# Cross attention with heads 0 and 2 first, and the square sums of the turned residual in the second MLP set

## The chip, the cores and the metric

The kernel runs on one core of one Trainium2 chip. The metric is the device time of one execution in microseconds (us): 706.7 is the median of three executions of the kernel before (706.44, 706.7 and 707.56). The profile was taken in a further execution. The engines are named as in the profile: PE multiplies matrices, PEld is its weight load, DVE and ACT work element by element, POOL does a few such steps and issues some transfers, SP issues the others.

## The reference

One decoder block over 512 tokens of width 1024, in float32, with a memory of 256 tokens. Two mixers side by side, cross attention to the memory, an MLP with squared ReLU, and a norm ahead of each. The change touches what follows the mixers:

```python
hc = rms_norm(x, g_cross[l])
mem_n = rms_norm(mem, g_mem[l])
x = x + memory_cross_attention(hc, mem_n, w_cq[l], w_ckv[l], w_co[l])
hm = rms_norm(x, g_mlp[l])
x = x + jnp.square(jax.nn.relu(hm @ w_up[l])) @ w_down[l]
return rms_norm(x, g_final)
```

`memory_cross_attention` has 4 heads of width 256: q = h w_cq, scores against 256 keys, a softmax, the product with the values, and w_co.

## The kernel before

A tile has 128 partitions. Activations lie transposed, 8 tiles of 128 features by 512 tokens. Each float32 operand is split into a high and a low part (`split`, L118: ACT casts the high part in L120, DVE subtracts it in L121), and every product is three matmuls, high by high, high by low, low by high (`mm3`, L113, so that the PE rows of the profile are nearly all L114, L115 and L116). A matmul over 256 columns that follows others of its kind starts 0.12 us after the one before, one over 512 columns 0.23 us after it. PE executes in the order in which the program is written. The other engines' instructions are put in order by a planner at build time, which takes an instruction ahead of others written earlier if it is ready sooner by its own estimate; on the chip each engine then keeps that order. Waits between engines are put in for every dependency, also where a buffer is used anew.

`tick` (L333) counts pieces of PE work: `tile_mm` ticks once for 3 matmuls of 512 columns, `block_product` once for 6 of 256 columns. `after(n, fn)` queues a function for n ticks from now; it is written into PE's order at that tick. `flush` writes out what is still queued.

**The query projection.** `cross_query(n)` makes the queries of heads 2n and 2n+1 with seven block products in place of eight (`seven`, L849). Its result has four quadrants: "11" and "12" are the first head with tokens 0 to 255 and 256 to 511, "21" and "22" are the second head with the same halves. Each of the seven products is 24 matmuls, 4 ticks. In `ORDER` "11" is finished after the fourth product (A12), "22" after the fifth (s3), "12" after the sixth (s4), and "21" after the seventh (A22). `finish` takes a quadrant from a PSUM tile to its two parts in the tile `s`: by a `split`, or, where the sign is negative ("22" and "21"), by ACT in L889 and DVE in L890. So the first head of each set is complete one product ahead of the second. The three PSUM tiles x, y, z have the tag `sc`, of which there are three buffers; "21" is read from y.

**Cross attention.** `cross_scores(h)` (L769) has two steps j, each of 12 matmuls into one PSUM tile: j = 0 are tokens 0 to 255, j = 1 the others. After each come a maximum on DVE (L780, L784), two exponentials on ACT (L785), a reciprocal (L786) and two scalings on ACT (L789). `cross_transpose(h)` (L793) turns the result by 8 PE transposes and splits it into `mfac` tiles. `cross_out(h)` (L805) multiplies it with the values in two steps of 6 matmuls over 512 columns, each into an `acc` or the `av` tile, and splits the result into `xg`, the operand of the output projection. The two scores of the first set are written into the second `cross_query`: at tick 2 head 1, at tick 7 head 0. After the second `cross_query` come, in PE's order: scores of 3, out of 1, scores of 2, transposes of 3, out of 0, out of 3, and then the output projection `co` with the transposes of 2 at its tick 2 and the out of 2 at its tick 7. `projection` (L603) starts with the input tiles that are there (`early`) for three output tiles, and adds the `late` ones when they are made.

**The MLP.** Eight up sets of seven block products each and four down products alternate (two sets, one down). The first set has its own order, `FIRST_ORDER`: A11, s1, A12, s2, s4, s3, A22. After s1, s2 and s3 ACT copies a PSUM tile aside (L857, L859, L865), and a later product goes on in the tile that was copied. `finish` there is a ReLU and a square on ACT (L998, L999). Meanwhile the residual is turned so that tokens lie on partitions: `turn(i, t)` (L934), written into PE's order at ticks 5 to 8 (i = 0) and 10 to 13 (i = 1) of the first set, makes 4 PE transposes, one copy by ACT (L939) into a `vr` buffer, and a square sum on ACT (`square_sum`, L931, the work being in L932). The `vr` buffers are those of the residual itself, so that no copy of i = 0 can be written before the fourth turn has read it. After the last turn DVE combines the sums (L943 to L946); they scale the down products (L954).

Of the kernel before, what the change touches and what calls it, by code (L numbers as in the profile page):

```python
# [21 lines left out]
NT = T // P  # L22
# [10 lines left out]
MEMIN, EARLY, LATE = 16, [4, 5, 6, 0, 1], [2, 7, 3]  # L33
WARM = 8
ON_POOL = (1, 3, 5, 7), (1, 3, 5)
STAT1, STATM, TURN = 16, 20, 5
RIGHT_START, RIGHT_SPACE = 12, 10
CO_ORDER = 0, 4, 1, 5, 2, 6, 3, 7
PARTS = "A11", "A12", "A21", "A22"
# [12 lines left out]
def block_kernel(ctx: ExitStack, tc: tile.TileContext, x0g, xT, memT, wv, wm, wst, wcq, wdn, wckv, wpool, vecs, csts, idn, gfin, out):  # L52
# [18 lines left out]
    def nm(s):  # L71
        uid[0] += 1
        return f"{s}_{uid[0]}"
# [7 lines left out]
    def sb(tag, shape, bufs, dt=F32):  # L81
        if tag in MID_TAGS and not late:
            return mid["pool"].tile(shape, dt, tag=tag, name=nm(tag), bufs=bufs)
        if tag in STAGE_TAGS and not late:
            return stage.tile(shape, dt, tag=tag, name=nm(tag), bufs=bufs)
        p = apool if tag in EARLY_TAGS else late["pool"] if tag in LATE_TAGS else pool
        return p.tile(shape, dt, tag=tag, name=nm(tag), bufs=bufs)

    def tmp(dt=F32):
        return sb("tmp", [P, T], 3 if late else 10, dt)  # L90

    def small(n=1):
        return sb("small", [P, 4], 24)[:, :n]

    def pair(tag, bufs):
        return sb(tag, [P, 2, T], bufs, F32R)

    def ps(tag, bufs):
        return psum.tile([P, T], F32, tag=tag, name=nm(tag), bufs=bufs)

    def acc():
        return ps("acc", 2)
# [10 lines left out]
    def mm3(o, lh, ll, rh, rl, start, stop, free=False):  # L113
        nc.tensor.matmul(o, lh, rh, start=start, stop=False, skip_group_check=free)  # L114
        nc.tensor.matmul(o, lh, rl, start=False, stop=False, skip_group_check=free)  # L115
        nc.tensor.matmul(o, ll, rh, start=False, stop=stop, skip_group_check=free)  # L116


    def split(hi, lo, src, eng=V):
        S.copy(hi, src)  # L120
        eng.tensor_tensor(lo, src, f(hi), op=ALU.subtract)  # L121
# [172 lines left out]
    def after(steps, fn, *args):  # L294
        heapq.heappush(due, (clock[0] + steps, uid[0], fn, args))
        uid[0] += 1

    def run_due():
        while due and due[0][0] <= clock[0]:
            _, _, fn, args = heapq.heappop(due)  # L300
            fn(*args)
# [6 lines left out]
    def flush():  # L308
        while due:
            clock[0] = max(clock[0], due[0][0])  # L310
            run_due()

    def tile_mm(o, w, rhs, ks=range(KC), first=True, last=True):
        ks = list(ks)
        for n, k in enumerate(ks):
            c = slice(k * P, (k + 1) * P)
            mm3(o, w[0][:, c], w[1][:, c], rhs[k][0], rhs[k][1],
                first and n == 0, last and n == len(ks) - 1)
            tick()
# [33 lines left out]
    def W(*key):  # L353
        return weights(where[key])
# [248 lines left out]
    def projection(key, rhs, early, late, done, between=None, order=range(KC)):  # L603
        held = []
        for m in order[:3]:
            w = W(key, m)
            o = ps("sc", 3)
            tile_mm(o, w, rhs, early, True, False)
            held.append((o, w))
        if between:  # L610
            between()
        for m, (o, w) in zip(order, held):
            tile_mm(o, w, rhs, late, False, True)
            done(m, o)
        for m in order[3:]:
            o = acc()
            tile_mm(o, W(key, m), rhs, early + late)
            done(m, o)
# [148 lines left out]
    cross_o = {}  # L767

    def cross_scores(h, tag, bufs):  # L769
        es = []  # L770
        for j in range(NT // 2):
            o = ps(tag, bufs)
            for b in range(2):
                i = 2 * j + b
                tb = slice(i * P, (i + 1) * P)
                for c in range(2):
                    q, k = st["cq", 2 * h + c], st["mk", 2 * h + c]
                    mm3(o[:, b * M:(b + 1) * M], q[0][:, tb], q[1][:, tb], k[0], k[1], c == 0, c == 1)
            mx, sm = small(2), small(2)
            V.tensor_reduce(mx, o.rearrange("p (b m) -> p b m", b=2), axis=AX.X, op=ALU.max, negate=True)  # L780
            e = tmp()
            for b in range(2):
                c, r = slice(b * M, (b + 1) * M), st["r1"][2 * j + b]
                V.tensor_tensor(mx[:, b:b + 1], mx[:, b:b + 1], r, op=ALU.mult)  # L784
                S.activation(e[:, c], o[:, c], AF.Exp, bias=mx[:, b:b + 1], scale=r, accum_out=sm[:, b:b + 1])  # L785
            V.reciprocal(sm, sm)  # L786
            for b in range(2):
                c = slice(b * M, (b + 1) * M)
                S.activation(e[:, c], e[:, c], AF.Copy, scale=sm[:, b:b + 1])  # L789
            es.append(e)  # L790
        st["p", h] = es

    def cross_transpose(h):  # L793
        pt = pair("mfac", 6), pair("mfac", 6)
        for j, e in enumerate(st["p", h]):
            tr = ps("tr", 2)
            for c in range(MT):
                for b in range(2):
                    nc.tensor.transpose(tr[:, (2 * c + b) * P:(2 * c + b + 1) * P],
                                        e[:, b * M + c * P:b * M + (c + 1) * P], ident)  # L800
            src = tr.rearrange("p (c t) -> p c t", c=MT)
            split(pt[0][:, :, j * M:(j + 1) * M], pt[1][:, :, j * M:(j + 1) * M], src)
        st["pt", h] = pt

    def cross_out(h):  # L805
        pt = st["pt", h]
        for dc in range(2):
            o = ps("av", 1) if (h, dc) in ((0, 0), (3, 1)) else acc()
            m = 2 * h + dc
            c = slice((m % 4) * P, (m % 4) * P + P)  # L810
            for i in range(MT):
                vh, vl = st["mv", m // 4, i]
                mm3(o, vh[:, c], vl[:, c], pt[0][:, i, :], pt[1][:, i, :], i == 0, i == MT - 1)
            pr = pair("xg", 8)
            split(pr[:, 0, :], pr[:, 1, :], o)
            cross_o[m] = (pr[:, 0, :], pr[:, 1, :])
# [59 lines left out]
    def cross_query(n):  # L876

        def store(m, p):
            st["cq", m] = p

        q = quads("s", 6, store, 4 * n)

        def finish(c, t, sign):
            hi, lo = q[c]
            t = two(t)
            if sign > 0:
                split(hi, lo, t)
            else:
                S.activation(hi, t, AF.Copy, scale=sign)  # L889
                V.scalar_tensor_tensor(lo, t, sign, f(hi), op0=ALU.mult, op1=ALU.subtract)  # L890

        seven("cq", n, rcross, finish, *(ps("sc", 3) for _ in range(3)), tmp(), tmp())

    cross_query(0)
    after(2, cross_scores, 1, "acc", 2)
    after(7, cross_scores, 0, "acc", 2)
    after(23, cross_transpose, 1)
    after(26, cross_transpose, 0)
    cross_query(1)
    flush()  # L900
    cross_scores(3, "sc", 3)
    cross_out(1)
    cross_scores(2, "sc", 3)
    cross_transpose(3)
    cross_out(0)
    cross_out(3)
    after(2, cross_transpose, 2)
    after(7, cross_out, 2)


    right = Right(G_MLP, "mix", 8, "s", 6)
# [12 lines left out]
        first.close()  # L924
        late["pool"] = ctx.enter_context(tc.tile_pool(name="late", bufs=1))

    projection("co", cross_o, [0, 1, 2, 3, 6, 7], [4, 5], done_co, renew, CO_ORDER)
    sums = sb("sums", [P, 32], 1)
    rows = {}

    def square_sum(t, i, col):  # L931
        S.activation(tmp(), rows[t, i], AF.Square, accum_out=sums[:, col:col + 1])  # L932

    def turn(i, t):  # L934
        o = ps("tr", 2) if t % 2 else acc()
        for j in range(4):
            nc.tensor.transpose(o[:, j * P:(j + 1) * P], res[4 * i + j][:, t * P:(t + 1) * P], ident)
        rows[t, i] = sb("vr", [P, T], 8)
        S.copy(rows[t, i], o)  # L939
        square_sum(t, i, NT * i + t)  # L940
        if i and t == NT - 1:
            v = sums[:, :NT]
            V.tensor_tensor(v, v, sums[:, NT:2 * NT], op=ALU.add)  # L943
            V.tensor_scalar(v, v, 1.0 / D, EPS, op0=ALU.mult, op1=ALU.add)
            V.reciprocal(sums[:, 2 * NT:3 * NT], v)
            V.tensor_scalar(sums[:, 6 * NT:7 * NT], sums[:, 2 * NT:3 * NT], -1.0, None, op0=ALU.mult)  # L946

    for i in range(2):
        for t in range(NT):
            after(TURN + (NT + 1) * i + t, turn, i, t)  # L950

    def gather(t, i, o, c=slice(T), minus=False):
        y, o, n = rows[t, i][:, c], o[:, c], (6 if minus else 2) * NT + t
# [249 lines left out]
```

## Time and profile before

The profiled execution took 702.63 us, of which the span from the first to the last instruction is 700.8; the median of the three executions without a profile is 706.7.

| | DVE | ACT | POOL | PEld |
|---|---|---|---|---|
| busy us in the span | 549.2 | 478.1 | 91.1 | 603.7 |
| share of the span | 78% | 68% | 13% | 86% |

The stages around the change, in us from the span's start:

| stage | from | to |
|---|---|---|
| second `cross_query`, with the scores of the first | 280.60 | 309.7 |
| scores, transposes and outs up to `co` | 309.7 | 329.6 |
| `co` | 329.6 | 376.9 |
| first up set | 376.9 | 401.9 |
| second up set | 401.9 | 421.9 |
| the rest of the MLP and the final norm | 421.9 | 700.8 |

A row of the timeline gives start, duration, engine, line, operation, the tiles (output first, then inputs), shapes and a count; at its end, in brackets, stands how long the engine had been idle and what released it. Durations of matmuls overlap, so their starts tell the pace. The windows view gives a stretch, its length, and for each engine the busy time and the number of instructions in it; then the granted PE clock as a share of full speed, the busy share of the transfer engines and GB/s.

### The profile page before, as it was taken

The numbers are of one execution on the slowest core, as the hardware profiler recorded it, in microseconds if no ns is written. First come the engines' busy times: TensorE is split into PE (matmuls) and PEld (weight loads), VectorE is DVE, ScalarE is ACT, GpSimd is POOL, SyncE is SP. The second block draws the span as 40 slices with busy tenths as digits, with TensorE's granted clock in tenths as the row PEclk, the third lists the DMA queues.
The fourth block names the chain that finished last, engine by engine and source line by source line (L and its number), as shares of the span: only waits on it lengthen the run. The fifth ranks groups of instructions, "written<-read, shape, count | busy, mean of one in ns | idle before, by whom it ended". The sixth has DMA issues, their size and how long they took to land.

```text
span 700.8 us, 10715 instructions
## 1 busy us (share of the span) xinstructions
PE 684.7 (98%) x4024; PEld 603.7 (86%) x4024; DVE 549.2 (78%) x824; ACT 478.1 (68%) x783; POOL 91.1 (13%) x87
## 2 busy tenths in 40 slices
PE   9999999999999999989999999999999999999995
PEld 6888788788889989988889998899988998899884
DVE  6597989987577996675388589868898689867996
ACT  7498999569646865757367977457853777358753
POOL 0044102543200000000100001101100001101100
PEclk9999999999999999999999999999999999999998
DMA  8543124125483546230664388876788488867713
GB/s 307 173 121 120 61 79 147 61 72 176 167 248 126 175 154 184 55 121 1 193 198 99 112 211 210 247 204 167 182 226 222 157 219 211 229 191 228 151 43 120
DMA packets 32995, 111.56 MB, mean 159 GB/s; under 512 B 3728, under 2 KB 4368, under 8 KB 32944
## 3 DMA queue, kind: packets, MB, share of 16 engines
q1 hardware_dynamic: 26416, 87.42, 36.5%
q0 software_dynamic: 6384, 23.20, 18.7%
q8 instruction: 31, 0.51, 0.3%
q10 hardware_dynamic: 144, 0.26, 0.1%
q14 instruction: 20, 0.16, 0.1%
HBM read 106.68 MB, written 2.10 MB: 155 GB/s over the span
## 4 chain that ended last, share of the span: by engine, by line
PE 83%; ACT 7%; DVE 5%; DMA 2%; issue 1%; POOL 0%; SPq 0%; DVEq 0%; ACTq 0%; POOLq 0%
PE acc L114 14%; PE acc L116 14%; PE acc L115 14%; PE sc L114 10%; PE sc L116 10%; PE sc L115 9%; PE tr L114 2%; PE tr L116 2%; PE tr L115 2%; ACT whi L120 2%; DMA mraw<-wcq 1%; DVE wlo L121 1%; ACT tmp L476 1%; DMA wraw<-wv 1%; PE sc L414 1%
## 5 line engine op out<-in xcount | busy, mean ns | idle before, releaser
L121 DVE TENSOR_TENSOR wlo<-wraw,whi 128x1024 fp32r<-128x1024 f32 (+1 forms) x80 | 98.0, 1227 | 24.6 <-ACT whi L120 24.5
L120 ACT CAST whi<-wraw 128x1024 fp32r<-128x1024 f32 (+1 forms) x80 | 82.3, 1031 | 47.1 <-PE acc L115 14.5
L121 DVE TENSOR_TENSOR wlo<-mraw,whi 128x1024 fp32r<-128x1024 f32 x58 | 70.6, 1221 | 34.3 <-ACT whi L120 34.3
L120 ACT CAST whi<-mraw 128x1024 fp32r<-128x1024 f32 x58 | 61.0, 1051 | 48.8 <-PE acc L116 12.3
L114 PE MATMUL acc<-xg,whi 128*128 128x512 f32 x200 | 80.1, 400 | 0.0
L116 PE MATMUL acc<-xg,wlo 128*128 128x512 f32 x200 | 78.2, 391 | 0.0
L115 PE MATMUL acc<-xg,whi 128*128 128x512 f32 x200 | 77.9, 390 | 0.0
L120 ACT CAST mhl<-mraw 128x1024 fp32r<-128x1024 f32 x32 | 33.6, 1053 | 26.2 <-PE sc L115 8.9
L121 DVE TENSOR_TENSOR mhl<-mraw,mhl 128x1024 fp32r<-128x1024 f32 x32 | 38.9, 1221 | 14.7 <-ACT mhl L120 14.7
L114 PE MATMUL sc<-mix,whi 128*128 128x256 f32 (+1 forms) x160 | 48.0, 300 | 0.0
L116 PE MATMUL sc<-mix,wlo 128*128 128x256 f32 (+1 forms) x160 | 47.4, 296 | 0.0
L115 PE MATMUL sc<-mix,whi 128*128 128x256 f32 (+1 forms) x160 | 47.3, 295 | 0.0
L116 PEld LDWEIGHTS acc<-xg,wlo 128*128 128x128 f32 x200 | 37.5, 188 | 8.3
L114 PEld LDWEIGHTS acc<-xg,whi 128*128 128x128 f32 x200 | 37.6, 188 | 7.2
L115 PEld LDWEIGHTS acc<-xg,whi 128*128 128x128 f32 x200 | 37.7, 188 | 7.0
L114 PE MATMUL acc<-s,whi 128*128 128x256 f32 x144 | 40.3, 280 | 0.0
L116 PE MATMUL acc<-s,wlo 128*128 128x256 f32 x144 | 40.2, 279 | 0.0
L115 PE MATMUL acc<-s,whi 128*128 128x256 f32 x144 | 40.2, 279 | 0.0
L181 POOL DMA_DIRECT2D mraw<-wst x16 | 13.8, 865 | 185.2 <-DMA mraw<-wst 86.5
L120 ACT CAST xg<-raws 128x1024 fp32r<-128x1024 f32 x28 | 29.4, 1049 | 12.3 <-PE acc L115 6.1
L121 DVE TENSOR_TENSOR xg<-raws,xg 128x1024 fp32r<-128x1024 f32 x28 | 33.9, 1218 | 4.8 <-ACT xg L120 4.8
L181 POOL DMA_DIRECT2D mraw<-wdn x16 | 13.8, 864 | 155.1 <-ACT raws L998 61.6
(399 smaller groups left out, 2184.7 us busy)
## 6 DMA issues: line engine op xcount, KB each, us to landing
wraw<-wm SPq DMA_DIRECT2D x36, 512.0 KB, 3.3
mraw<-wst SPq DMA_DIRECT2D x24, 512.0 KB, 4.4
mraw<-wdn SPq DMA_DIRECT2D x24, 512.0 KB, 4.3
mraw<-wdn POOLq DMA_DIRECT2D x24, 512.0 KB, 6.8
wraw<-wckv SPq DMA_DIRECT2D x16, 512.0 KB, 3.4
mraw<-wst POOLq DMA_DIRECT2D x16, 512.0 KB, 7.1
wraw<-wst SPq DMA_DIRECT2D x16, 512.0 KB, 5.3
wraw<-wdn SPq DMA_DIRECT2D x16, 512.0 KB, 5.0
```

Of the source, the lines that this page charges most:

```text
L114: nc.tensor.matmul(o, lh, rh, start=start, stop=False, skip_group_check=free)
L115: nc.tensor.matmul(o, lh, rl, start=False, stop=False, skip_group_check=free)
L116: nc.tensor.matmul(o, ll, rh, start=False, stop=stop, skip_group_check=free)
L120: S.copy(hi, src)
L121: eng.tensor_tensor(lo, src, f(hi), op=ALU.subtract)
L181: nc.gpsimd.dma_start(r, part(key, then), accum_op=ALU.add)
L414: nc.tensor.matmul(o[i], xg[k][0][:, tbs[i]], wh[:, c], start=k == 0, stop=False)
L476: S.activation(e[:, :n], e[:, :n], AF.Exp, bias=mn, scale=-1.0, accum_out=sm[:, c:c + 1])
```

## The change

In cross attention heads 0 and 1 change places, and so do 2 and 3, in scores, transposes and outs; with them the choice of PSUM tile in `cross_out` and the lists of early and late input tiles of `co`. The number and the shapes of all instructions stay. The square sums of the turned residual, with the DVE steps that combine them, become a function of their own, `turned`, queued for ticks 30, 32, ... 44, counted as the turns are. A set has 28 ticks, so these lie in the second up set. Nothing that is moved issues a transfer.

```diff
-STAT1, STATM, TURN = 16, 20, 5
+STAT1, STATM, TURN, SQUARES = 16, 20, 5, 30
...
-            o = ps("av", 1) if (h, dc) in ((0, 0), (3, 1)) else acc()
+            o = ps("av", 1) if (h, dc) in ((1, 0), (2, 1)) else acc()
...
     cross_query(0)
-    after(2, cross_scores, 1, "acc", 2)
-    after(7, cross_scores, 0, "acc", 2)
-    after(23, cross_transpose, 1)
-    after(26, cross_transpose, 0)
+    after(2, cross_scores, 0, "acc", 2)
+    after(7, cross_scores, 1, "acc", 2)
+    after(23, cross_transpose, 0)
+    after(26, cross_transpose, 1)
     cross_query(1)
     flush()
+    cross_scores(2, "sc", 3)
+    cross_out(0)
     cross_scores(3, "sc", 3)
+    cross_transpose(2)
     cross_out(1)
-    cross_scores(2, "sc", 3)
-    cross_transpose(3)
-    cross_out(0)
-    cross_out(3)
-    after(2, cross_transpose, 2)
-    after(7, cross_out, 2)
+    cross_out(2)
+    after(2, cross_transpose, 3)
+    after(7, cross_out, 3)
...
-    projection("co", cross_o, [0, 1, 2, 3, 6, 7], [4, 5], done_co, renew, CO_ORDER)
+    projection("co", cross_o, [0, 1, 2, 3, 4, 5], [6, 7], done_co, renew, CO_ORDER)
...
         S.copy(rows[t, i], o)
+
+    def turned(t, i):
         square_sum(t, i, NT * i + t)
         if i and t == NT - 1:
...
             after(TURN + (NT + 1) * i + t, turn, i, t)
+            after(SQUARES + 2 * (NT * i + t), turned, t, i)
```

## The prediction

> **What bounds the kernel now.** I read the page's shares first, then PE's waits, then the timeline around each wait.
>
> ```profile
> PE 684.7 (98%) x4024; PEld 603.7 (86%) x4024; DVE 549.2 (78%) x824; ACT 478.1 (68%) x783; POOL 91.1 (13%) x87
> ```
>
> PE is busy 98% of the span, so only two things can shorten it: fewer PE instructions, which the change doesn't bring, or fewer gaps in PE. PE's waits, by what released it:
>
> ```profile
> PE sc L114 <- ACT s L889: 1.6, 1, 1.6
> PE acc L116 <- DVE s L890: 1.1, 1, 1.1
> PE sc L116 <- DVE s L890: 0.9, 1, 0.9
> PE sc L114 <- ACT raws L859: 0.8, 1, 0.8
> PE acc L937 <- ACT vr L939: 0.4, 1, 0.4
> PE av L114 <- DVE xg L121: 0.3, 1, 0.3
> ```
>
> The columns are total us, times, longest. L889 and L890 finish quadrants "22" and "21" of the queries: the first three waits are cross attention taking the head whose quadrant "21" comes last. L859 is an ACT copy in the first up set, where the square sums stand. Behind that set PE waits for nothing:
>
> ```profile
> 422.00:690.00 268.00, 268.00 (x1668) 242.22 (x1667) 222.09 (x227) 169.40 (x213) 28.53 (x33) 1.00 0.71 188
> ```
>
> In these 268 us PE is busy throughout. What is gained ahead of them should therefore arrive at the end in full, as the weights' buffers come free at PE's own pace.
>
> **Part 1: the first scores, in the second query.** First PE, then DVE:
>
> ```profile
> 282.16 0.28 PE L115 MATMUL acc<-mix,s 128*128 128x256 f32 x1
> 283.54 0.39 PE L116 MATMUL acc<-mix,s 128*128 128x256 f32 x1 [1.10 <-DVE s L890]
> 283.77 0.28 PE L114 MATMUL acc<-mix,s 128*128 128x256 f32 x1
> ```
> ```profile
> 281.06 0.69 DVE L121 TENSOR_TENSOR s<-tmp,s 128x512 fp32r<-128x512 f32 x1
> 282.80 0.68 DVE L890 SCALAR_TENSOR_TENSOR s<-sc,s 128x512 fp32r<-128x512 f32 x1
> ```
>
> At the pace of 0.12 the two steps from 282.16 to 283.77 would take 0.24 us; they take 1.61. The stall costs 1.37. Head 0 needs "11" for its first 12 matmuls and "12" for the next 12. "12" is complete at 281.75 (281.06 + 0.69), ahead of 282.04, where the scores start. The stall goes. Late next would be head 1 at tick 7, some 6 us on, for which L890 ended at 283.48. **Gain 1.37.**
>
> **Part 2: behind the second query.** PE from the last product on, the windows of the slow stretch, and the engines that release PE:
>
> ```profile
> 309.43 0.28 PE L116 MATMUL sc<-mfac,wlo 128*128 128x256 f32 x1
> 311.27 0.39 PE L114 MATMUL sc<-mix,s 128*128 128x256 f32 x1 [1.56 <-ACT s L889]
> 312.63 0.39 PE L116 MATMUL sc<-mix,s 128*128 128x256 f32 x1 [0.86 <-DVE s L890]
> ...
> 313.81 0.38 PE L116 MATMUL sc<-mix,s 128*128 128x256 f32 x1
> ...
> 317.58 0.39 PE L114 MATMUL acc<-mfac,mix 128*128 128x512 f32 x1
> ```
> ```profile
> 313.80:315.00 1.20, 1.20 (x8) 1.20 (x7) 0.74 (x2) 0.00 (x0) 0.00 (x0) 0.52 0.73 283
> 315.00:316.50 1.50, 1.50 (x9) 1.50 (x8) 0.24 (x3) 1.20 (x4) 0.00 (x0) 0.50 0.00 0
> ```
> ```profile
> 309.68 1.04 ACT L120 CAST whi<-wraw 128x1024 fp32r<-128x1024 f32 x1 [0.71 <-ACT mfac L120]
> 310.63 0.59 ACT L889 ACTIVATE s<-sc 128x512 fp32r<-128x512 f32 x1
> ```
> ```profile
> 308.42 0.68 DVE L121 TENSOR_TENSOR s<-tmp,s 128x512 fp32r<-128x512 f32 x1
> 311.89 0.68 DVE L890 SCALAR_TENSOR_TENSOR s<-sc,s 128x512 fp32r<-128x512 f32 x1
> ```
>
> From 309.43 to 317.58 PE starts 25 steps over 256 columns and 3 over 512, which at the usual pace is 25 x 0.119 + 3 x 0.233 = 3.68 us. It takes 8.15, so 4.47 are lost: 1.56 and 0.86 as waits, 0.5 in stopping and restarting, and about 1.5 because from 313.8 to 317.2 the granted clock is 0.5 and the matmuls start 0.21 apart. "12" of head 2 is ready at 309.10, and "11" earlier: nothing of the data holds head 2 up at 309.55.
>
> What could hold it up is its PSUM tile, for of the three `sc` buffers y is still being read by L889 and L890. In the program built of the kernel before, the tile y of the second query lies in bank 2 and the two score tiles that follow in banks 4 and 3: the planner hands out buffers that are already free. So I take no wait. L889 and L890 now run beside the scores of head 2 and the out of head 0, and head 3 needs them only some 5.7 us later.
>
> What is late next: DVE. The maximum over the first score tile is ready near 311.1 and queues behind the weight subtraction of 310.75 to 311.98 and L890, to 312.5; the first exponential follows near 313.45, 2.3 us behind its matmuls, where before (313.97 to 315.20) it was 1.2. PE on the other hand loses its slow stretch. ACT's work up to `co`:
>
> ```profile
> 316.55:329.60 13.05, 12.75 (x70) 10.74 (x70) 7.58 (x20) 10.18 (x27) 0.00 (x0) 0.97 0.01 1
> 315.20 0.56 ACT L785 ACTIVATE tmp<-sc,small,rrow 128x256 f32<-128x256 f32 x1 [3.99 <-DVE small L784]
> ...
> 322.76 0.56 ACT L785 ACTIVATE tmp<-sc,small,rrow 128x256 f32<-128x256 f32 x1 [2.03 <-DVE small L784]
> 328.08 0.50 PE L114 MATMUL av<-mfac,mix 128*128 128x512 f32 x1 [0.30 <-DVE xg L121]
> ```
>
> With the 1.20 of the window before it ACT has 11.4 us of work there. PE from the end of the first score tile to `co` took 313.98 to 329.58, or 15.6; without the slow clock (1.5) and the stall at 328.08 (0.6, of which 0.3 is in the list of waits) it is 13.5. ACT needs 2.3 + 11.4 = 13.7 if it never idles, and 2.5 more with the idle times that it had (0.23, 0.22 and 2.03). A new wait of PE here is thus between 0 and 2.5 us. I take 0.6, as large as the stall at 328.08 that this queue already causes, which I leave in place. **Gain 4.47 - 0.6 = 3.9.**
>
> A rule weighed here: the Trainium skill, page "TensorE: Matmul & The Clock Gate", section "Why this matters for your kernels", says that the clock falls to half after PE has been idle for one window, and advises no gaps over some 3 us. The trace differs: gaps of 1.56 and 0.86 preceded the drop. By the row the drop goes with the gaps; by the page it has another cause, stays, and part 2 is worth 1.5 less. That is rival b.
>
> **Part 3: the square sums.** PE and ACT in the first set, ACT's square sums as one group (window 376 to 424), and the windows of the two halves:
>
> ```profile
> 395.08 0.28 PE L116 MATMUL sc<-mix,mhl 128*128 128x256 f32 x1
> 396.15 0.39 PE L114 MATMUL sc<-s,mhl 128*128 128x256 f32 x1 [0.79 <-ACT raws L859]
> 396.38 0.28 PE L115 MATMUL sc<-s,mhl 128*128 128x256 f32 x1
> ```
> ```profile
> 394.83 0.70 ACT L932 ACTIVATE tmp<-vr 128x512 f32<-128x512 f32 x1
> 395.46 0.64 ACT L859 COPY raws<-sc 128x512 f32<-128x512 f32 x1
> ...
> 411.43 0.58 ACT L859 COPY raws<-sc 128x512 f32<-128x512 f32 x1
> ```
> ```profile
> L932 ACT ACTIVATE tmp<-vr 128x512 f32<-128x512 f32 x8 | 5.1, 678 | 0.0
> ```
> ```profile
> 386.40:401.90 15.50, 14.71 (x124) 14.50 (x125) 7.72 (x12) 15.48 (x34) 0.07 (x1) 1.00 0.31 103
> 401.90:421.90 20.00, 20.00 (x171) 19.99 (x170) 16.92 (x17) 16.11 (x22) 2.52 (x3) 1.00 0.82 199
> ```
>
> 395.08 to 396.38 should be 0.24 and is 1.30: 1.06 lost, since L859 could run from 392.5 (s2 ends) and ran at 395.46. Five square sums stand ahead of it; one takes about 0.62 of ACT with its readout, so it moves some 3 us earlier and the stall goes. The wait of 0.4 at the fifth turn stays: no square sum precedes its copy.
>
> Where the sums go: 8 x 0.62 = 4.9 us on ACT. The second set leaves ACT 20.00 - 16.11 = 3.9 free, and 4.9 come: 1.0 too much if all land there. Against that, ACT was full in the first window (15.48 of 15.5), so it now enters the second set without its backlog, and the planner takes ready work early (the weight cast of 309.68 is written behind all the scores and outs, yet ran ahead of L889). A square sum on ACT holds up the weight casts and the copies L855 to L859 behind it, and PE behind these; each has 1.4 us or more to spare (L859 of the second set ran at 411.43 and its tile is written again at 413.3). Bounds: 0 and 1.0. I take 0.3, half a square sum once ahead of a copy. The combining steps on DVE are four of about 0.17; they come near 414, and their reader L954 first runs at 431.69:
>
> ```profile
> 431.69 0.74 DVE L954 SCALAR_TENSOR_TENSOR vr<-sc,sums,vr 128x512 f32<-128x512 f32 x1
> ```
>
> **Gain 1.06 - 0.3 = 0.8.**
>
> No part moves a transfer, so the queues of SP and POOL keep their order; only their start follows PE.
>
> **Sum.** 1.37 + 3.9 + 0.8 = 6.0 us. On the profiled execution that is 702.63 - 6.0 = 696.6. The median without a profile is 4.07 above the profiled time; I take the same gain there: **700.7 us**. With no new waits it would be 6.9 and 699.8; if the two old stalls of 0.4 and 0.3 went as well, about 699.
>
> **Rivals.**
>
> a) ACT's queue at part 2 takes 2.5 us in place of 0.6. For it: the 13.7 against 13.5. Against: the idle 2.03 was itself waiting for a PE that was late. Gain 4.1: 702.6.
>
> b) The slow clock stays, or the runs without a profile never had it. For it: one drop was seen, and the executions differ by 1.1 us among themselves. Against: it follows the two gaps directly. Gain 4.5: 702.2.
>
> c) The change doesn't do in part 2 what it says, since the second score tile gets y's buffer and waits for L890 until 312.63 while its turn comes at 310.98: 1.65 lost. Against: the banks. Gain 4.35: 702.4.
>
> d) The square sums take back nearly all: each of eight delays a copy or cast that PE waits for, 8 x 0.62 = 4.9 of 6.0: 705.6. Against: ACT's free 3.9 us in the second set and about 4.9 in the first.
>
> e) Slower: d, and with gaps like those of part 2 the clock halves again. It needs PE to wait for ACT at each of the seven products, which begins where ACT's work in a product exceeds the product: 16.11/7 = 2.30, with 0.70 of square sums 3.00, against 20.00/7 = 2.86. Three slow stretches of 1.5 on top of 4.9 are 9.4, against 6.0 gained: 3.4 slower, 710.1. Against: the excess is 0.14 a product, and the sums needn't all run there.
>
> **How the numbers follow.** My forecast 0.56, a 0.13, b 0.13, c 0.04, d 0.08, e 0.06. About 0.2% (1.4 us) is what a measurement of this kernel can tell from no change. Forecast, a, b and c are faster by more: 0.86. d is within it: 0.08. e is slower: 0.06. The range from 699.2 (no new waits and one old stall less) to 704.0 (a and b together with some of d) leaves out d and e and the edges of the forecast.
>
> **What would show it.** Right: no PE wait for L889 or L890; clock 1.00 throughout 309 to 320; no wait for L859; PE's first `co` matmul some 5 us earlier; L932 behind 398. Wrong: a wait for L890 on a matmul of head 2 (c); waits for `mfac` or `xg` above 1 us ahead of `co` (a); clock 0.5 again (b); PE waiting for ACT casts or copies between 396 and 420 (d, e). A gain above 7.5 us or a loss would mean that I have missed a bound.

## The result, and the profile after

| | before | after |
|---|---|---|
| median of four executions, us | 706.93 | 698.71 |
| range | 706.44 to 707.56 | 696.98 to 700.70 |
| profiled execution (span) | 702.63 (700.8) | 697.03 (695.2) |

The ratio is 0.9884, with an interval of 0.9848 to 0.9921. The forecast was 700.7 and the range began at 699.2, so the change gained more than it allowed for, by 0.5 us. Executions of both kernels come in two kinds, some us apart, and after's four are two of each (696.98, 697.03; 700.39, 700.70); what parts them is shown below.

The page's shares and PE's waits of the kernel after, as those shown of before:

```profile
PE 682.4 (98%) x4024; PEld 601.9 (87%) x4024; DVE 548.9 (79%) x824; ACT 477.6 (69%) x783; POOL 91.0 (13%) x87
```
```profile
PE acc L137 <- DVE tmp L134: 1.2, 1, 1.2
...
PE sc L114 <- ACT raws L859: 0.8, 1, 0.8
...
PE acc L114 <- ACT tmp L785: 0.5, 1, 0.5
PE acc L937 <- ACT vr L939: 0.4, 1, 0.4
```

The three waits for L889 and L890 are gone. The one for L859, which part 3 was to remove, is there as before, and one for L785 is new. PE's timeline at the places of the three parts (start, duration, engine, line, output and inputs, shape; the wait in brackets):

```profile
281.82 0.28 PE L115 MATMUL acc<-mix,s 128*128 128x256 f32 x1
...
288.82 0.39 PE L114 MATMUL acc<-mix,s 128*128 128x256 f32 x1 [0.52 <-ACT tmp L785]
...
308.50 0.28 PE L116 MATMUL sc<-mfac,wlo 128*128 128x256 f32 x1
308.62 0.28 PE L114 MATMUL sc<-mix,s 128*128 128x256 f32 x1
...
312.20 0.39 PE L114 MATMUL acc<-mfac,mix 128*128 128x512 f32 x1
...
390.55 0.39 PE L114 MATMUL sc<-s,mhl 128*128 128x256 f32 x1 [0.78 <-ACT raws L859]
```

Each row has its counterpart in the prediction's rows of before, and the difference of the starts is the lead that after has there: 0.34 us at the first scores (282.16), 0.93 at the last product of the second query (309.43), 5.38 at the fourth step of the first out (317.58) and 5.60 at the stall of the first up set (396.15). The spans differ by 5.6. So part 1 brought 0.59, part 2 brought 4.45, part 3 nothing; the first 0.34 lies ahead of the change and is no part of it. The last 0.22 is the old stall at 328.08, which is shorter: that step took 0.70 us before (327.38 to 328.08) and takes 0.48 after (322.00 to 322.48).

Behind the second query the scores of head 2 start 0.12 us after the last product, without a wait for the PSUM tile, and the clock stays up. A window of the kernel after (busy time by engine, then the clock, the share of the transfer engines and GB/s):

```profile
309.00:320.00 11.00, 11.00 (x76) 10.09 (x75) 8.43 (x22) 8.87 (x25) 0.00 (x0) 1.00 0.25 91
```

ACT in the first up set of the kernel after shows what became of part 3:

```profile
389.23 0.70 ACT L932 ACTIVATE tmp<-vr 128x512 f32<-128x512 f32 x1
...
389.86 0.64 ACT L859 COPY raws<-sc 128x512 f32<-128x512 f32 x1
390.32 0.70 ACT L932 ACTIVATE tmp<-vr 128x512 f32<-128x512 f32 x1
```

The square sums are written 25 to 31 ticks later, but the planner put them back where they were: one stands right ahead of L859, as at 394.83 before.

### The profile page after: what moved, and what is told of

Same layout as the page of the kernel before. It is cut to its first block, busy times and chain, and to the rows that moved or that the text cites. A ratio compares the mean times of both kernels' runs of the same rounds, so it can differ in the third digit from the quotient of the medians.

```text
span 695.2 us, 10715 instructions
## 1 busy us (share of the span) xinstructions
PE 682.4 (98%) x4024; PEld 601.9 (87%) x4024; DVE 548.9 (79%) x824; ACT 477.6 (69%) x783; POOL 91.0 (13%) x87
## 4 chain that ended last, share of the span: by engine, by line
PE 82%; ACT 8%; DVE 5%; issue 2%; DMA 1%; POOL 1%; SPq 0%; DVEq 0%; ACTq 0%
PE acc L114 14%; PE acc L116 14%; PE acc L115 13%; PE sc L114 9%; PE sc L115 9%; PE sc L116 9%; PE tr L114 2%; PE tr L116 2%; PE tr L115 2%; ACT whi L120 1%; DVE wlo L121 1%; PE sc L414 1%; ACT tmp L476 1%; ACT tmp L785 1%; PE sc L416 1%
```

## The experiments

### Which part brings what

Four kernels have parts of the change alone. `e1_heads_only` is the kernel after with `square_sum` back in `turn`; `e2_squares_only` is the kernel before with `turned`; `e3_first_pair` and `e4_second_pair` are the kernel before with one pair of heads exchanged. The edits of the last two, against before:

```diff
# e3_first_pair
-    after(2, cross_scores, 1, "acc", 2)
-    after(7, cross_scores, 0, "acc", 2)
-    after(23, cross_transpose, 1)
-    after(26, cross_transpose, 0)
+    after(2, cross_scores, 0, "acc", 2)
+    after(7, cross_scores, 1, "acc", 2)
+    after(23, cross_transpose, 0)
+    after(26, cross_transpose, 1)
# e4_second_pair
-            o = ps("av", 1) if (h, dc) in ((0, 0), (3, 1)) else acc()
+            o = ps("av", 1) if (h, dc) in ((0, 0), (2, 1)) else acc()
...
+    cross_scores(2, "sc", 3)
+    cross_out(1)
     cross_scores(3, "sc", 3)
-    cross_out(1)
-    cross_scores(2, "sc", 3)
-    cross_transpose(3)
+    cross_transpose(2)
     cross_out(0)
-    cross_out(3)
-    after(2, cross_transpose, 2)
-    after(7, cross_out, 2)
+    cross_out(2)
+    after(2, cross_transpose, 3)
+    after(7, cross_out, 3)
...
-    projection("co", cross_o, [0, 1, 2, 3, 6, 7], [4, 5], done_co, renew, CO_ORDER)
+    projection("co", cross_o, [0, 1, 2, 3, 4, 5], [6, 7], done_co, renew, CO_ORDER)
```

> The heads exchanged, the square sums left in their old place. Theory: the planner had put the square sums back where they were, so this is the changed kernel over again: 5.6 us less than before between executions of one kind, the stall on L859 at 390.5 with 0.8 us in both. Rival: the square sums are worth the 0.8 us forecast, then this is 0.8 us slower than the changed kernel.

> The square sums moved alone, the heads as before. Theory: same time as before within 0.5 us, L932 at 387 to 398 as before and the wait for L859 of 0.8 us still there. Rival: 0.8 to 1.1 us faster, no wait for L859.

> Heads 0 and 1 exchanged in the scores and transposes of the second query alone; heads 2 and 3 and all outs as before. Theory: the stall of 1.37 us near 283 goes and one of about 0.6 us on L785 near 289 comes, so 0.7 to 0.8 us faster; the two gaps near 311 stay. If the slow clock follows the gaps, it stays as well near 313, up to its place against the clock's own windows; if it has another cause its place and length won't follow them.

> Heads 2 and 3 exchanged alone, the scores of heads 0 and 1 as before. Theory: part 2 alone, 4.5 us faster if the slow clock goes with the gaps, 3.0 if the slow clock has another cause; the wait of 1.1 us near 283 stays.

Measured, beside the kernel before on the same chip (median 707.56 of 31 executions):

| | median us | range | executions | ratio and interval |
|---|---|---|---|---|
| `e1_heads_only` | 700.48 | 696.92 to 701.49 | 8 | 0.9932 (0.9894 to 0.997) |
| `e2_squares_only` | 707.43 | 701.83 to 708.37 | 12 | 1.0 (0.997 to 1.003) |
| `e3_first_pair` | 704.66 | 701.89 to 705.87 | 12 | 0.9976 (0.9953 to 1.0) |
| `e4_second_pair` | 703.29 | 697.4 to 704.5 | 12 | 0.9939 (0.9911 to 0.9967) |

Part 3 does nothing: on every engine the instructions of `e2_squares_only` stand in the order of before, and those of `e1_heads_only` in the order of after. The theories of both runs hold: `e2_squares_only` takes the time of before, with the wait of 0.8 for L859 still there, and `e1_heads_only` is after measured again. One of its eight executions is of the faster kind and seven lie between 699.81 and 701.49; the twelve of both together have a median of 700.4. The medians of the two pairs alone are 2.9 and 4.3 us below 707.56, and together 7.2, against 7.1 for both pairs: they add up. (The quotients of the medians differ from the ratios, since the times of each kernel fall into two groups, but lie within the intervals.) The 4.3 of the second pair is near the 4.5 expected if the slow clock goes. The 2.9 of the first pair is far more than the 0.7 to 0.8 expected; the next section shows where it comes from.

### Two kinds of execution: a transfer lands early or late

All these kernels have two groups of times: 701.8 and 704.2 to 708.4 in `e2_squares_only`, 697.4 and 701.6 to 704.5 in `e4_second_pair`. The profiled execution of before (702.63) was one of the faster kind, so before was run once more, unchanged, for another profile:

> The kernel before once more, for one more profiled execution of it. Theory (its executions differ by when the accumulating transfer of the second query lands): if it comes out near 707, the weight cast waits over 5 us for the transfer, PE has a wait of about 3 us for L889 and of about 2 for L890 near 284 to 288, and the clock is 0.5 for some 3.4 us behind them; if it comes out near 702, the cast waits 2.3 us and PE 1.1, as in the first profile. Rival: it is near 707 with the first profile's wait of 1.1 and the time lost elsewhere.

It took 707.91 us, with a span of 706.1, and has what the theory says for that time, except that the half clock lasts twice as long. ACT's timeline, first in the first profile of before, then in this one:

```profile
278.85 1.05 ACT L120 CAST whi<-mraw 128x1024 fp32r<-128x1024 f32 x1 [2.34 <-DMA mraw<-wcq]
279.80 0.61 ACT L120 CAST s<-tmp 128x512 fp32r<-128x512 f32 x1
280.80 0.60 ACT L889 ACTIVATE s<-sc 128x512 fp32r<-128x512 f32 x1 [0.39 <-PE sc L116]
```
```profile
282.96 1.04 ACT L120 CAST whi<-mraw 128x1024 fp32r<-128x1024 f32 x1 [6.71 <-DMA mraw<-wcq]
283.91 0.61 ACT L120 CAST s<-tmp 128x512 fp32r<-128x512 f32 x1
284.43 0.59 ACT L889 ACTIVATE s<-sc 128x512 fp32r<-128x512 f32 x1
```

The weight cast belongs to product s1 of the second query, which PE needs only later. Its weight `mraw` is the sum of two parts, the second of which POOL's queue adds by a transfer. The quadrants "12" (`s<-tmp`) and "21" (L889) stand behind this cast on ACT, and in the second profile they start 4.1 and 3.6 us later. The transfers issued between 268 and 290, as issue, size and median us to landing; again the first profile of before, then the second:

```profile
mraw<-wcq POOLq DMA_DIRECT2D x2, 512.0 KB, 6.3
```
```profile
mraw<-wcq POOLq DMA_DIRECT2D x2, 512.0 KB, 9.3
```

PE in the second profile of before, with windows of it:

```profile
281.67 0.28 PE L116 MATMUL sc<-xg,wlo 128*128 128x256 f32 x1
285.07 0.38 PE L114 MATMUL acc<-mix,s 128*128 128x256 f32 x1 [3.12 <-ACT s L889]
285.30 0.28 PE L115 MATMUL acc<-mix,s 128*128 128x256 f32 x1
287.66 0.58 PE L116 MATMUL acc<-mix,s 128*128 128x256 f32 x1 [2.08 <-DVE s L890]
...
293.58 0.36 PE L116 MATMUL sc<-xg,wlo 128*128 128x256 f32 x1
...
316.23 0.28 PE L116 MATMUL sc<-mfac,wlo 128*128 128x256 f32 x1
318.07 0.39 PE L114 MATMUL sc<-mix,s 128*128 128x256 f32 x1 [1.56 <-ACT s L889]
...
319.43 0.39 PE L116 MATMUL sc<-mix,s 128*128 128x256 f32 x1 [0.86 <-DVE s L890]
...
322.88 0.39 PE L114 MATMUL acc<-mfac,mix 128*128 128x512 f32 x1
```
```profile
287.00:293.50 6.50, 5.84 (x27) 5.84 (x28) 4.50 (x9) 2.25 (x5) 0.00 (x0) 0.50 0.00 0
316.00:320.00 4.00, 1.58 (x11) 1.17 (x10) 2.92 (x4) 1.54 (x2) 0.00 (x0) 1.00 0.43 146
320.00:324.00 4.00, 4.00 (x28) 3.67 (x27) 1.75 (x6) 1.86 (x6) 0.00 (x0) 1.00 0.30 116
```

At the place of part 1 the stall is 3.40 - 0.12 = 3.28, then 2.36 - 0.12 = 2.24, and from 287.66 to about 293.6 the clock is half, which at starts 0.213 apart in place of 0.119 costs 2.6. That is 8.1 us where the first profile lost 1.37. At the place of part 2 the same two waits of 1.56 and 0.86 are there, but the clock stays at 1.00: from 316.23 to 322.88 it takes 6.65 us against 8.15, so 1.5 less. 8.1 - 1.37 - 1.5 = 5.2, against 5.3 between the spans.

In the kernel after a late landing costs less, since the first scores now need "12" and not "21". ACT and PE of `e1_heads_only`, whose profiled execution (700.59) is of that kind:

```profile
282.34 1.05 ACT L120 CAST whi<-mraw 128x1024 fp32r<-128x1024 f32 x1 [6.34 <-DMA mraw<-wcq]
```
```profile
283.95 0.39 PE L114 MATMUL acc<-mix,s 128*128 128x256 f32 x1 [0.83 <-ACT s L120]
285.30 0.38 PE L116 MATMUL acc<-mix,s 128*128 128x256 f32 x1 [0.84 <-DVE s L121]
285.52 0.28 PE L114 MATMUL acc<-mix,s 128*128 128x256 f32 x1
285.64 0.28 PE L115 MATMUL acc<-mix,s 128*128 128x256 f32 x1
...
291.86 0.39 PE L114 MATMUL acc<-mix,s 128*128 128x256 f32 x1 [1.54 <-ACT tmp L785]
...
311.98 0.28 PE L116 MATMUL sc<-mfac,wlo 128*128 128x256 f32 x1
```

The last matmul of its second query starts at 311.98, against 316.23 in before with a late landing, a lead of 4.25 us. The matmul ahead of the first scores already has a lead of 0.25 (281.42 against 281.67), so part 1 is worth 4.00, where it was 0.59 with an early landing. Like with like, the change gains 700.8 - 695.2 = 5.6 with an early and 706.1 - 698.8 = 7.3 with a late landing.

The two pairs alone fit this. The profiled execution of `e3_first_pair` has the early landing (6.3 us) and takes 701.89, or 0.74 less than the first of before, as was expected; its waits of 1.6 and 0.9 for L889 and L890 near 310, and the slow clock behind them, stay. That of `e4_second_pair` has the late one (9.2 us): those two waits are gone, and in place of the expected 1.1 near 283 it has 3.02 and 2.08, as before has with a late landing. Its 703.29 is 4.6 less than 707.91.

If that is the cause, the spread goes when the quadrants no longer stand behind the cast. `e12_before_cast` does this to the kernel before, `e8_cast_behind` to the kernel after; nothing else is changed:

```diff
         for j in range(i, i + 3 + far // 4):
+            if j == where["cq", 1, "s1"] and i < where["cq", 1, "A11"]:
+                continue
...
-                prep(j)
+                behind = j == where["cq", 1, "s1"] and j not in made
+                with tc.issue_after(st["negated"]) if behind else nullcontext():
+                    prep(j)
...
-                S.activation(hi, t, AF.Copy, scale=sign)
+                st["negated"] = S.activation(hi, t, AF.Copy, scale=sign).ins
```

> The changed kernel with the weight cast of the second query's product s1, which waits for a transfer, queued on ACT behind the last quadrant of the first query (L889) in place of ahead of it. Theory: the two kinds of execution, 3.5 us apart, come from this transfer's landing, some 5.5 or 9.4 us after its issue, with the quadrants waiting behind the cast in ACT's queue; then the slow kind all but goes and the median falls from about 700.5 to 697 to 698. Rival: the spread has another source and stays, median 700 to 701.

> The kernel before, with only the preparation of product s1 of the second query moved behind the negated cast. Theory (the timed runs of before are 4 to 5 us above its profiled execution because the weight cast waits for an accumulating transfer and holds up the quadrant casts behind it): median about 702, spread under 2 us, ratio about 0.992. Rival (the offset has another cause, and the cast matters only in the changed order): median stays at about 707.

`e8_cast_behind`: 698.03 (697.58 to 698.64, 5 executions), ratio 0.9886 (0.9846 to 0.9926). `e12_before_cast`: 701.66 (699.24 to 702.61, 12), ratio 0.9934 (0.9909 to 0.9959), where before on the same chip had 707.15 (700.88 to 708.36, 17). ACT and the transfers of `e12_before_cast`:

```profile
278.30 0.62 ACT L120 CAST s<-tmp 128x512 fp32r<-128x512 f32 x1 [2.15 <-DVE tmp L872]
280.45 0.60 ACT L893 ACTIVATE s<-sc 128x512 fp32r<-128x512 f32 x1 [1.53 <-PE sc L116]
282.15 1.05 ACT L120 CAST whi<-mraw 128x1024 fp32r<-128x1024 f32 x1 [1.10 <-DMA mraw<-wcq]
```
```profile
mraw<-wcq POOLq DMA_DIRECT2D x2, 512.0 KB, 8.9
```

The transfer lands late and the cast still waits for it, but no quadrant does, and PE's waits for L889 and L890 at the first scores are gone. In ACT's order this cast is the only instruction that changed its place against before. A late landing still costs something: PE waits 0.18 and 0.85 us for the readouts of the first score tiles (L785, numbered L789 there), and 0.32 and 0.85 in `e8_cast_behind`, whose profile has a late landing too (8.4 us):

```profile
291.03 0.39 PE L114 MATMUL acc<-mix,s 128*128 128x256 f32 x1 [0.85 <-ACT tmp L789]
```

The upper group of times is gone in both kernels. So the cause is shown, and a move of one cast that isn't in the change takes 5.5 us from the median of before. The times of `e12_before_cast` still spread over 3.4 us and not under 2; these small waits and the slow clock behind part 2's waits, which its profile has, could make that up, but no run parts them. With the cast moved in both kernels, the heads are worth 701.66 - 698.03 = 3.6 us (on two chips, on which before differs by 0.2).

### The new wait for L785

> The changed kernel with the scores of head 1 at tick 9 in place of 7 of the second query, 12 matmuls later. Theory: the new wait for L785 near 289 (0.52 in the fast executions, 1.5 in the slow ones) goes in the fast and shrinks by 1.4 in the slow. Rival: PE waits as long for the next thing, same time.

```diff
-    after(7, cross_scores, 1, "acc", 2)
+    after(9, cross_scores, 1, "acc", 2)
```

698.59 us (698.32 to 700.72, 5), ratio 0.9901 (0.9864 to 0.9938): within the spread of after, so the times don't decide between the two. Its profiled execution has a late landing, and there the L785 wait of `e1_heads_only` (1.54) is gone, as the theory says. But the half clock is back, behind waits hardly longer than there. PE and a window of `e7_tick9`:

```profile
284.83 0.39 PE L114 MATMUL acc<-mix,s 128*128 128x256 f32 x1 [1.08 <-ACT s L120]
...
286.18 0.56 PE L116 MATMUL acc<-mix,s 128*128 128x256 f32 x1 [0.84 <-DVE s L121]
```
```profile
286.30:289.60 3.30, 3.30 (x16) 3.30 (x17) 2.74 (x4) 1.04 (x1) 0.00 (x0) 0.50 0.00 0
```

Tick 9 and the moved cast together:

> Changed kernel, the preparation of product s1 of the second query moved behind the negated cast (L889) as in the run before it, and the scores of head 1 at tick 9 in place of 7. Theory (what is left in that query is the copy of the two first score tiles' readout queued behind casts, .32 + .85 us there): about 697 us, all timed runs within some 1.5 us of each other, no PE wait between 280 and 300. Rival (the wait only moves with the scores): the same as with the cast moved alone, 698.0.

697.27 (696.45 to 697.5, 5), ratio 0.988 (0.9841 to 0.992). PE waits nowhere between 276 and 325 in its profile, and the times lie within 1.1 us, as the first theory says. That profile has an early landing (6.4 us), though; with a late one the same order has a wait of 0.85 there, as `e11_spread` shows below. The 0.8 below the cast alone is small beside the ranges, but these don't overlap.

### The square sums

> The changed kernel with the square sums held behind an ACT instruction of the second up set by an order edge, so that the planner can't take them early. Theory: the stall on L859 near 390 goes and 1.06 us with it, against the changed kernel; new waits of PE in the second set between 0 and 1.0. Rival: the stall on L859 isn't due to the square sums and stays; then the same time as the changed kernel.

```diff
-STAT1, STATM, TURN, SQUARES = 16, 20, 5, 30
+STAT1, STATM, TURN, SQUARES = 16, 20, 5, 33
...
-                S.copy(y, x)
+                st["mark", key, n] = S.copy(y, x).ins
...
-        square_sum(t, i, NT * i + t)
+        with tc.issue_after(st["mark", "up", 1]):
+            square_sum(t, i, NT * i + t)
```

701.31 (698.51 to 702.13, 9), ratio 0.9922 (0.9897 to 0.9948): no gain on the 700.4 of after's order. Forced into the second set behind its first copy, the square sums run between 402.39 and 411.53, and the wait near 390 is gone, so the square sums do cause it. In its place PE waits in the second set, for 1.67 us where the theory allowed 1.0 at most; PE and ACT of `e5_squares_late`:

```profile
411.15 0.39 PE L114 MATMUL sc<-s,whi 128*128 128x256 f32 x1 [1.67 <-ACT raws L859]
```
```profile
409.50 0.19 ACT L932 ACTIVATION_READ_ACCUMULATOR tmp<-vr 128x1 f32 x1
410.52 0.58 ACT L859 COPY raws<-sc 128x512 f32<-128x512 f32 x1
```

> The changed kernel without the square sums of the turned residual (L932 in the turns; constants stand in for the sums, so the scale of the MLP's contribution differs). It bounds what any placing of them can bring. Theory: 1.06 us less than the changed kernel, no wait for L859; the wait of 0.4 for L939 stays. Rival: more than 1.5 less, if ACT's load in the two sets costs PE elsewhere too.

```diff
+    V.memset(sums, 1.0)
...
-        square_sum(t, i, NT * i + t)
```

699.1 (695.97 to 700.51, 6), ratio 0.9892 (0.9854 to 0.9929). The stall at L859 is gone, and the wait for L939 is still there. Its two faster executions (695.97, 696.12) lie 0.9 to 1.1 below those of after, about the 1.06 of the stall; by these two, the square sums cost no more than that in all.

> The run e9, and the eight square sums spread over the second up set, two behind each of its four finishing squares on ACT, where the planner can't take them forward. Theory (the 1.06 us at L859 in the first set are owed to the square sums ahead of it, and two at a time fit beside a product of the second set): 1 us below e9, about 696. Rival (any copy of the second set that stands behind them is late by as much, as when all eight came together): 0 to 0.7 us above e9.

```diff
-            after(SQUARES + 2 * (NT * i + t), turned, t, i)
...
-            S.activation(home[c], home[c], AF.Square)
+            squared = S.activation(home[c], home[c], AF.Square).ins
+            if n == 1:
+                for _ in range(2):
+                    j = len(st.setdefault("squares", []))
+                    st["squares"].append(j)
+                    with tc.issue_after(squared):
+                        turned(j % NT, j // NT)
```

696.3 (695.19 to 696.78, 5), ratio 0.9866 (0.9826 to 0.9905): 1.0 below `e9_cast_tick9`, as the theory says, and the lowest median of all, though the ranges overlap (`e9_cast_tick9` begins at 696.45). The windows of the first set, of `e9_cast_tick9` and then of `e11_spread`:

```profile
386.00:400.00 14.00, 13.21 (x113) 13.00 (x112) 9.90 (x15) 13.28 (x25) 0.86 (x1) 1.00 0.33 74
```
```profile
386.00:400.00 14.00, 14.00 (x122) 14.00 (x121) 9.07 (x11) 10.80 (x17) 0.86 (x1) 1.00 0.30 69
```

The wait of 0.79 at L859 (numbered L863 there) is gone, and none comes up in the second set. The spans of the two profiles are nevertheless the same, 694.6 and 694.7, because that execution of `e11_spread` had the late landing (8.8 us, against 6.4), which in this order still costs one short wait, for a copy that is L855 in the kernel before. The subtraction of the late weight on DVE starts at 283.46, against 282.13 in `e9_cast_tick9`; the maximum over the first scores stands behind it, and the readouts and this copy behind that on ACT:

```profile
290.13 0.38 PE L114 MATMUL sc<-mfac,whi 128*128 128x256 f32 x1 [0.85 <-ACT sc L859]
```

## Why the prediction was right or wrong

**The step that failed** is "The median without a profile is 4.07 above the profiled time; I take the same gain there". The 4.07 was no constant: it came from the late landing, a larger stall at the very place of part 1, so part 1 is worth 4.00 in such an execution and 0.59 in the other. The gain there is 7.3 and not 6.0. After's own offset is also smaller, 698.8 - 695.2 = 3.6, and its four executions were half of each kind, which by chance put their median, 698.71, between the groups. With the twelve of the same order, 700.4, the forecast of 700.7 would have been close, but out of a wrong split: on the profiled execution 696.6 was forecast and 697.03 came. The trace of before had the hint in it, a cast waiting 2.34 us for a transfer with two needed quadrants queued behind it; the prediction looked at the quadrants' rows from 281.06 on and not at what stood ahead of them.

**Part 1.** The first stall went as said. Of the 1.37, 0.59 came: the step "Late next would be head 1 at tick 7" asked only for the quadrants. PE waits there for head 1's PSUM tile, because head 0's exponentials (L785) now stand on ACT behind a weight cast and a copy. `e7_tick9`, with the scores two ticks later, has no such wait, even with a late landing.

**Part 2.** Right. There is no wait for L889 or L890 and none for y's buffer (rival c is out), and none of the 0.6 charged to ACT's queue appeared (rival a is out): 4.45 of the 4.47 came, and 0.22 of the stall at 328.08 that was left in place. The 1.5 for the slow clock hangs on the execution: of five profiles with these two waits, four have the half clock behind them (before, `e2_squares_only`, `e3_first_pair`, `e12_before_cast`), and the second profile of before doesn't. So rival b's "the runs without a profile never had it" is true of some executions. Of the 63 executions of before that ran beside the experiments, four have a mean granted clock of 0.998, as the profile of after has, and take 700.06 to 700.88; how many of the others had the slow clock at this place is open.

**Part 3.** 0 in place of 0.8. The text said itself that "the planner takes ready work early" and did not draw the conclusion that it would undo the move. Rivals d and e, by which the sums "take back nearly all" or more, fell too: without the sums altogether the kernel gains about 1 us, and forced late in a lump they cost the 1.67 at L859.

**Sum.** On the profiled execution 0.59 + 4.45 + 0 of the parts, 0.34 ahead of the change and 0.2 between 317.58 and 396.15 make 5.6, against 6.0. The errors of parts 1 and 3 were 0.8 each, and that of part 2 was 0.55 the other way.

## What to carry to other kernels

Before a profiled time is set against a median, look for what differs between executions: an in-order engine whose early instruction waits for a transfer passes the transfer's spread on to all that is queued behind it, needed or not, and moving that one instruction behind the urgent ones was worth more to the median of before (5.5 us) than the profile showed as a stall (1.37). When an edit moves work in a program that a planner puts in order, read the built order first: here it put the square sums back, and only a dependency on a later instruction kept them late. Where PE's next piece moves up, ask for its PSUM tile too, not for its operands alone. A wait of PE can also cost clock behind it, and whether it does can differ between two executions of one kernel.

## What was not expected of the hardware

- The same kernel's transfers from POOL's queue landed after 6.3 us in one execution and 9.3 in another; in the fourteen profiles it is 6.3 or 6.4 in five and 8.3 to 9.3 in nine. Why is open.
- Waits of the same length don't always halve the clock, and the traces show what decides. In each of them the granted clock changes on a grid of 3.413 us: the stretches between its steps last whole multiples of that. In the first profile of before full speed lasts 307.20 us (90 of them) up to 313.86, and half speed one; in the second, full speed lasts 279.89 (82) up to 286.92, and half speed two. Against the kernel the grid lies at another place in each execution. Windows along it, two of the first profile and two of the second (the first number behind the length is PE's busy time):

```profile
310.44:313.86 3.42, 1.73 (x12) 1.53 (x13) 1.82 (x2) 0.78 (x2) 0.00 (x0) 1.00 0.43 134
313.86:317.27 3.41, 3.41 (x16) 3.31 (x16) 1.57 (x5) 1.83 (x6) 0.00 (x0) 0.50 0.24 94
```
```profile
314.22:317.64 3.42, 2.29 (x20) 2.08 (x18) 2.97 (x5) 2.33 (x5) 0.00 (x0) 1.00 0.37 126
317.64:321.05 3.41, 2.12 (x15) 1.92 (x16) 1.85 (x3) 0.37 (x1) 0.00 (x0) 1.00 0.45 168
```

In the first, most of the waits of 1.56 and 0.86 falls into one window, PE is busy for half of it, and the next window is at half speed. In the second the edge at 317.64 parts them, and the clock stays. In the fourteen profiles, each window at full speed with PE busy for 1.67 us or less was followed by half speed, and none with 1.80 or more; of the two in between, 1.73 was (the row above) and 1.69 was not (`e4_second_pair`, from 280.27). By these windows it's the busy share of a window that counts, and not the length of a gap: 0.91 and 0.84 us in one window halved the clock in `e6_no_squares` (busy 1.66, from 282.92), and 0.83 and 0.84 in two windows didn't in `e1_heads_only` (2.58 and 2.57, from 280.60). The Trainium skill, page "TensorE: Matmul & The Clock Gate", section "What's actually happening", gives a window of 3413 ns that runs freely, without regard to the kernel; the traces agree with it. The Trainium skill's advice that the prediction weighed, no gaps over some 3 us, doesn't cover this case: here gaps of under 1 us were enough.
